# Making the Indexer's high and low parts as the features leave PSUM, instead of splitting each head's stack

## The chip, the cores and the metric

The kernel runs on one core of a Trainium2 chip. The metric is the device time of one launch in microseconds (us). The engines are named as in the profile: PE (TensorE), DVE (VectorE), ACT (ScalarE), POOL (GpSimd) and SP (SyncE, which here only issues DMAs).

## The reference

One transformer block over 1024 tokens of width 1024. The part that matters here is the Indexer of the sparse attention: it scores every key for every query, and the 256 best keys per query are kept.

```python
h = modulate(x, sh1, sc1)
proj = h @ w_in[l]
(aq, ak, av, iq, ik, iw, gq, gk, ...) = jnp.split(proj, SPLIT_OFFSETS, axis=-1)
...
iw = iw * (IDX_HEADS ** -0.5 * IDX_DIM ** -0.5)          # 16 heads of 32
idx_logits = jnp.einsum('bqhd,bsd->bqhs', iqb, ik)
score = jnp.einsum('bqh,bqhs->bqs', iwb, jax.nn.relu(idx_logits)).astype(jnp.float32)
score = jnp.where(causal[None], score, -jnp.inf)
_, sel = lax.top_k(score, topk)                           # 256 of up to 1024
```

Behind it come the attention over the selected keys, a gated linear attention (GLA), two output projections, a layer norm, a mixture of 32 experts and a last layer norm.

## The kernel before

All matmuls that must keep float32 accuracy are made of three: a number is split into a high part (what the type fp32r keeps) and a low part (the rest), and `mm3` (lines 180 to 183) adds high x high, high x low and low x high.

The first stage makes the modulated activations, transposed, as eight high and eight low tiles of 128 features x 1024 tokens (`hTh`, `hTl`). The projection stage then goes through units of 256 columns of `w_in`. `unit_load` (L214) loads a unit's raw weights by SP's queue, and `convert` splits them in four pieces, the high part on ACT (L822) and the low part on POOL (L823), while the unit before is being multiplied. The order of the units is: the keys of the Indexer with other narrow columns (`first_unit`), two units of Indexer queries (`iq_tile`, four tiles of 128 rows, that is four heads each), four gate units, then the GLA units and the rest. `feat_group` makes half a tile (128 features x 512 tokens) with eight k-steps of three matmuls into a PSUM bank of the pool `pj`, which has two.

Beside the units run threads written as Python generators: `stack_work`, `idx_work`, later `topk_work` and the GLA's. A planner's clock `now` moves by 0.64 at each k-step of `feat_group` (`spend`), and at each move every thread whose due time has come puts its next instructions into the program; each `yield` says when the thread is due again. So the order of the instructions on PE, DVE, ACT and POOL is fixed by this clock when the program is written. SP's order is left to the framework.

The Indexer's data takes this way before the change. `iq_tile` copies each half tile from PSUM to SBUF on ACT (L478) and writes the tile to a DRAM buffer `diq` (L479); `first_unit` does the same with the keys (L442, L443). A head needs its 32 query rows four times, as a stack of 128 partitions: high, high, low, low against a key stack of high, low, high, low, so that one matmul adds all products. `stack_load` loads 32 rows from DRAM four times into a raw tile of 128 partitions (L424, two buffers). `high_low` copies the whole raw tile to the stack as high part (ACT, L429) and overwrites the lower half with raw minus high (POOL, L431). The key stack `iks` is made in the same way with two such subtractions. There are six stack buffers `iqs`, so a stack is made at most five heads ahead.

`idx_work` goes through the 16 heads, and in each through the eight query blocks i with (i + 1) x 128 keys: one or two matmuls of stack and key stack into `ips` (L495, three PSUM tiles), the relu on ACT into `ixr` (L497, three buffers), and on DVE `acc += relu * weight` (L504; for head 0 L501 and L502). It is planned 25% slower than n x 1.04 ns + 0.2 us for each block, 8.0 us of the planner's clock a head. When all gate units before the GLA are placed, `finish(idx)` puts in what is left, and the top-k (L522, L525, with a last pass L528 and L531) begins on DVE beside the GLA and the other units. At the stage's end `qk_unit` makes query and key parts on ACT, POOL and DVE (L758).

The transposes of the Indexer's per-token weights (L454) and all `ips` tiles take over the PSUM banks of the pool `pjx`, in which the first query tile's two halves were begun.

Of the kernel before, what the change touches and what calls it, by code (L numbers as in the profile page):

```python
# [10 lines left out]
F32 = mybir.dt.float32  # L11
F32R = mybir.dt.float32r
# [3 lines left out]
AF = mybir.ActivationFunctionType  # L16
OP = mybir.AluOpType
# [5 lines left out]
S = 1024  # L23
# [4 lines left out]
IH = 16  # L28
# [11 lines left out]
STK_W = 4.5  # L40
STK_M = 3.5
# [117 lines left out]
def block_kernel(ctx, tc, A, out, dbg=None, stop=99):  # L159
# [4 lines left out]
    V, SC, PE, GP, SY = nc.vector, nc.scalar, nc.tensor, nc.gpsimd, nc.sync  # L164

    const = ctx.enter_context(tc.tile_pool(name="const", bufs=1))
    dram = ctx.enter_context(tc.tile_pool(name="dram", bufs=1, space=DRAM))
# [12 lines left out]
    def mm3(ps, ah, al, bh, bl, first, last):  # L180
        PE.matmul(ps, ah, bh, start=first, stop=False)  # L181
        PE.matmul(ps, ah, bl, start=False, stop=False)  # L182
        PE.matmul(ps, al, bh, start=False, stop=last)  # L183
# [168 lines left out]
    now, dve = [0.0], [0.0]  # L352
# [8 lines left out]
    def spend(dt):  # L361
        now[0] += dt
        for s in list(streams):
            while s in streams and s[1] <= now[0]:
                resume(s)

    def start(gen, delay=0.0):
        streams.append([gen, now[0] + delay])
        return streams[-1]
# [9 lines left out]
    scp = vstk.enter_context(tc.tile_pool(name="sc", bufs=1, side="right"))  # L379
    acc = [scp.tile([128, (i + 1) * 128], F32, name=f"acc{i}") for i in range(NT)]  # L380

    diq = dram.tile([544, S], F32, name="diq")
    dqk = dram.tile([1024, S], F32, name="dqk")
    dob = dram.tile([512, S], F32, name="dob")
    dvec = dram.tile([H, 384], F32, name="dvec")
# [3 lines left out]
    def feat_group(w, m0, m, half, key=None):  # L389

        ps = begun.pop((key, half), None)
        k0 = 0 if ps is None else 4
        if ps is None:
            ps = pj.tile([128, 512], F32, name="pj")[:m]
        sl = slice(half * 512, half * 512 + 512)
        for k in range(k0, KT):
            mm3(ps, w[0][:, k, m0:m0 + m], w[1][:, k, m0:m0 + m], hTh[k][:, sl], hTl[k][:, sl],
                k == 0, k == KT - 1)
            spend(0.64)
        return ps, sl  # L400
# [11 lines left out]
    c0T = wp.tile([64, S], F32, name="c0T", bufs=1)  # L412
# [4 lines left out]
    ixw = idxs.enter_context(tc.tile_pool(name="ixw", side="right", bufs=2))  # L417
    ixr = idxs.enter_context(tc.tile_pool(name="ixr", side="right", bufs=3))
    iks = ix1.tile([128, S], F32R, name="iks")

    def stack_load(src, rows):
        raw = ixw.tile([128, S], F32, name="sraw")
        for r in range(0, 128, rows):
            SY.dma_start(raw[r:r + rows], src)  # L424
        return raw

    def high_low(dst, raw, low):

        SC.activation(dst, raw, AF.Copy)  # L429
        for r in low:  # L430
            GP.tensor_tensor(dst[r], raw[r], dst[r].bitcast(F32), op=OP.subtract)  # L431

    LOW64, LOW0 = slice(64, 128), slice(0, 64)

    stacks, written, heads = {}, {}, [0]

    ipp = []

    def first_unit(w):
        for half in range(2):  # L440
            ps, sl = feat_group(w, 0, 64, half, "k")
            SC.activation(c0T[:, sl], ps, AF.Copy)  # L442
        SY.dma_start(diq[512:544], c0T[0:32])  # L443
        written["k"] = now[0]

    def stack_work():

        raw = stack_load(diq[512:544], 32)
        yield STK_0
        for half in range(2):  # L450
            ps = ipp[0].tile([128, S], F32, name="ips")[:, :512].rearrange("p (t c) -> p t c", c=128)
            for q in range(4):
                t = half * 4 + q
                PE.transpose(ps[:, q, :64], c0T[:, t * 128:(t + 1) * 128], ident[:64, :64])  # L454
            V.tensor_scalar(iwt[:, half * 4:half * 4 + 4], ps[:, :, 48:64], 16 ** -0.5 * 32 ** -0.5, None, op0=OP.mult)
            now[0] += 0.3
            yield STK_K
        high_low(iks, raw, (slice(32, 64), slice(96, 128)))
        raws_ = {}
        for h in range(IH):  # L460
            for a in (h, h + 1):
                if a < IH and a not in raws_ and (a == h or a // 4 in written):
                    while a // 4 not in written:
                        yield 0.7
                    raws_[a] = stack_load(diq[a * 32:(a + 1) * 32], 32), now[0] + (STK_M if a % 4 < 2 else 0.0)
            while now[0] < raws_[h][1] + STK_W or heads[0] < h - 5:
                yield 0.6
            stacks[h] = ixs.tile([128, S], F32R, name="iqs")
            high_low(stacks[h], raws_[h][0], (LOW64,))
            written[h, "s"] = now[0]  # L470
            yield 1.0

    def iq_tile(w, m):

        f_ = ixw.tile([128, S], F32, name="iqf")
        for half in range(2):
            ps, sl = feat_group(w, (m % 2) * 128, 128, half, "q" if m == 0 else None)
            SC.activation(f_[:, sl], ps, AF.Copy)  # L478
        SY.dma_start(diq[m * 128:(m + 1) * 128], f_)  # L479
        written[m] = now[0]  # L480
        if m == 0:
            pjx.close()
            ipp.append(idxs.enter_context(tc.tile_pool(name="ipp", bufs=3, space=PSUM)))
            start(stack_work())

    def idx_work():
        for h in range(IH):
            while (h, "s") not in written or now[0] < written[h, "s"] + 2.6:
                yield 0.6
            for i in range(NT):  # L490
                n = (i + 1) * 128
                ps = ipp[0].tile([128, S], F32, name="ips")[:, :n]
                for c in range(0, n, 512):
                    e = min(c + 512, n)
                    PE.matmul(ps[:, c:e], stacks[h][:, i * 128:(i + 1) * 128], iks[:, c:e], start=True, stop=True)  # L495
                r = ixr.tile([128, S], F32, name="ixr")[:, :n]
                SC.activation(r, ps, AF.Relu)  # L497
                sc = iwt[:, i, h:h + 1]
                if h == 0:
                    if i:  # L500
                        V.tensor_scalar(acc[i][:, :n - 128], r[:, :n - 128], sc, None, op0=OP.mult)  # L501
                    V.scalar_tensor_tensor(acc[i][:, n - 128:], r[:, n - 128:], sc, causal, op0=OP.mult, op1=OP.add)  # L502
                else:
                    V.scalar_tensor_tensor(acc[i], r, sc, acc[i], op0=OP.mult, op1=OP.add)  # L504
                now[0] += n / 2400
                yield IDXF * (n * 1.04e-3 + 0.2)
            heads[0] = h + 1
# [305 lines left out]
    def convert(cols, dst):  # L813
        raw = unit_load(cols)
        yield 6.5
        dst.append(None)
        n = raw.shape[2]
        hi = wp.tile([128, KT, 256], F32R, name="whi")[:, :, :n]
        lo = wp.tile([128, KT, 256], F32R, name="wlo")[:, :, :n]
        dst[0] = (hi, lo)  # L820
        for k in range(0, KT, 2):
            SC.activation(hi[:, k:k + 2], raw[:, k:k + 2], AF.Copy)  # L822
            GP.tensor_tensor(lo[:, k:k + 2], raw[:, k:k + 2], hi[:, k:k + 2].bitcast(F32), op=OP.subtract)  # L823
            yield 2.2
# [4 lines left out]
    def units():  # L829
        yield lambda _, w: [iq_tile(w, m) for m in range(2)], 0, [(OFF_IQ, 256)]  # L830
        yield lambda _, w: [iq_tile(w, m) for m in range(2, 4)], 0, [(OFF_IQ + 256, 256)]
        for _ in range(NG0):
            yield gate()
        yield "gla", None, None
        for p in range(2):
            yield gla_unit_a, p, [(OFF_GQ + p * 128, 128), (OFF_GK + p * 128, 128)]
            yield gla_unit_v, p, [(OFF_GV + p * 256, 256)]
            yield gla_unit_r, p, [(OFF_GR + p * 256, 256)]
            while len(gates) > (NG1 if p == 0 else 0):
                yield gate()  # L840
            if p == 0:
                yield "steps", None, None
        for u in (1, 3):
            yield qk_unit, u, [(u * 256, 256)]
        yield "values", None, None
        for u in range(2):
            yield v_unit, u, [(OFF_AV + u * 256, 256)]
        yield "attention", None, None
        for u in (0, 2):
            yield qk_unit, u, [(u * 256, 256)]  # L850

    todo_ = list(units())
    work = [u for u in todo_ if u[2] is not None]
    idx = start(idx_work(), 10.0)
    first_unit(w0)
    ready, n, topk = [wiq[0]], 0, None
    for f, a, cols in todo_:
# [13 lines left out]
        else:  # L871
            n += 1
            nxt = []
            s = start(convert(work[n][2], nxt)) if n < len(work) else None
# [324 lines left out]
    rows = {}  # L1199
# [734 lines left out]
```

## Time and profile before

| | |
|---|---|
| median of 3 runs | 1417.73 us (1417.11 to 1421.07) |
| profiled execution | 1416.12 us |
| its span | 1414.3 us |
| mean granted clock of PE | 0.966 of full speed |
| busy: PE, DVE, ACT, POOL | 1314.1 (93%), 1167.2 (83%), 730.0 (52%), 484.0 (34%) us |
| DMA | 262.69 MB, mean 186 GB/s |

The profile is of one execution. Times in it count from the start of its span. A busy time is the union of the instructions of an engine, which overlap a little at their ends; matmuls are pipelined, and their ends are modelled, so their distance from start to start tells more than their length. The granted clock is a share of full speed: 1.00 is 2.4 GHz, and a mean between 0.5 and 1.00 is a mix with 1.2 GHz. The projection stage lies between about 65 and 662 us, and its Indexer part between 65 and 248 us.

### The profile page before, as it was taken

What the parts mean: (1) busy time and instruction counts of PE and PEld (TensorE: products, weight loads), DVE (VectorE), ACT (ScalarE), POOL (GpSimd) and SP (SyncE); (2) the same over time, 40 slices, a digit from 0 to 9 for tenths busy, and PEclk for the clock granted to TensorE, in tenths of its full rate; (3) what the DMA queues carried; (4) which work ended last, traced back from release to release, by engine and by line L of the source; (5) the groups of instructions that cost most, each with busy time, mean ns of one, the idle gap of its engine ahead of it and who ended that gap; (6) DMA issues with size and microseconds to landing.
All of it is one profiled execution on the core that took longest, in us unless ns stands there. A gap on an engine that the chain in (4) does not pass through costs nothing. (4 is left out here: it accounts for less than half of the span.)

```text
span 1414.3 us, 21326 instructions
## 1 busy us (share of the span) xinstructions
PE 1314.1 (93%) x7535; PEld 1057.3 (75%) x7535; DVE 1167.2 (83%) x2127; ACT 730.0 (52%) x1321; POOL 484.0 (34%) x492
## 2 busy tenths in 40 slices
PE   4988999999999999998989999989869999999975
PEld 2566778897889788996447768989758888888842
DVE  5638998997989799993878758788889999999947
ACT  2446776343234322223566644322348988898834
POOL 2465441275227522132455424311211222222114
PEclk9999999999999999999999999999859999999987
DMA  8454332121302123202774456837459999999964
GB/s 279 163 157 141 119 93 87 46 61 35 115 31 64 56 92 108 72 31 89 284 268 133 137 169 223 293 123 255 150 183 370 371 387 365 371 345 366 372 248 176
DMA packets 133375, 262.69 MB, mean 186 GB/s; under 512 B 20656, under 2 KB 71144, under 8 KB 131216
## 3 DMA queue, kind: packets, MB, share of 16 engines
q1 hardware_dynamic: 122336, 243.17, 49.3%
q0 software_dynamic: 9216, 16.80, 3.2%
q8 instruction: 60, 0.98, 0.3%
q10 hardware_dynamic: 1712, 1.32, 0.3%
q14 instruction: 51, 0.42, 0.1%
HBM read 229.61 MB, written 48.39 MB: 197 GB/s over the span
## 5 line engine op out<-in xcount | busy, mean ns | idle before, releaser
L1562 DVE TENSOR_TENSOR elo<-pg,ehi 128x1024 fp32r<-128x1024 f32 x188 | 219.1, 1220 | 17.5 <-ACT ehi L1557 13.3
L181 PE MATMUL pj<-hTh,whi 128*128 128x512 f32 (+1 forms) x528 | 211.3, 400 | 0.0
L182 PE MATMUL pj<-hTl,whi 128*128 128x512 f32 (+1 forms) x528 | 207.5, 393 | 1.9 <-DVE hTl L307 1.2
L183 PE MATMUL pj<-hTh,wlo 128*128 128x512 f32 (+1 forms) x528 | 207.2, 392 | 0.0
L1557 ACT ACTIVATE ehi<-pg 128x1024 fp32r<-128x1024 f32 x192 | 190.2, 1075 | 0.9 <-PE eph L183 0.9
L823 POOL TENSOR_TENSOR wlo<-raw,whi 128x512 fp32r<-128x512 f32 x84 | 111.8, 1344 | 208.8 <-ACT whi L822 199.8
L525 DVE MATCH_REPLACE8 acc<-m,acc 128x1024 f32<-128x1024 f32 (+2 forms) x192 | 167.8, 886 | 0.0
L522 DVE MAX8 m<-acc 128x8 f32<-128x1024 f32 (+2 forms) x192 | 163.0, 889 | 0.0
L504 DVE SCALAR_TENSOR_TENSOR acc<-ixr,iwt,acc 128x128 f32<-128x128 f32 (+3 forms) x120 | 127.2, 1115 | 15.5 <-ACT ixr L497 14.8
L181 PEld LDWEIGHTS pj<-hTh,whi 128*128 128x128 f32 (+1 forms) x528 | 98.9, 187 | 22.8 <-issue 1.9
L182 PEld LDWEIGHTS pj<-hTl,whi 128*128 128x128 f32 (+1 forms) x528 | 99.1, 188 | 22.4 <-DVE hTl L307 2.7
L183 PEld LDWEIGHTS pj<-hTh,wlo 128*128 128x128 f32 (+1 forms) x528 | 98.9, 187 | 22.7 <-issue 0.6
L181 PE MATMUL pj<-whi,hTh 128*128 128x256 f32 x384 | 111.8, 291 | 0.0
L182 PE MATMUL pj<-wlo,hTh 128*128 128x256 f32 x384 | 108.6, 283 | 0.0
L183 PE MATMUL pj<-whi,hTl 128*128 128x256 f32 x384 | 108.5, 283 | 0.0
L181 PE MATMUL eph<-ehi,xh 128*128 128x512 f32 x256 | 105.5, 412 | 0.0
L182 PE MATMUL eph<-elo,xh 128*128 128x512 f32 x256 | 102.6, 401 | 1.1 <-DVE elo L1567 1.1
L497 ACT ACTIVATE ixr<-ips 128x128 f32<-128x128 f32 (+7 forms) x128 | 80.3, 656 | 44.4 <-DVE acc L504 24.2
L183 PE MATMUL eph<-ehi,xl 128*128 128x512 f32 x256 | 102.3, 400 | 0.0
L1581 POOL DMA_INDIRECT xg<-dh,gidx x32 | 34.3, 1071 | 161.4 <-PE etp L1677 139.8
L181 PEld LDWEIGHTS pj<-whi,hTh 128*128 128x128 f32 x384 | 73.4, 191 | 6.8 <-issue 5.5
L181 PE MATMUL yps<-whi,pg 128*128 128x256 f32 x256 | 74.7, 292 | 0.2 <-ACT pg L1242 0.2
(321 smaller groups left out, 3195.2 us busy)
## 6 DMA issues: line engine op xcount, KB each, us to landing
pg<-in_w_exp_gate_dram SPq DMA_DIRECT2D x64, 512.0 KB, 13.1
pg<-in_w_exp_up_dram SPq DMA_DIRECT2D x64, 512.0 KB, 13.9
pg<-in_w_exp_down_dram SPq DMA_DIRECT2D x32, 1024.0 KB, 15.8
raw<-in_w_in_dram SPq DMA_DIRECT2D x20, 1024.0 KB, 5.4
wada<-in_w_ada_dram SPq DMA_DIRECT2D x16, 1024.0 KB, 5.7
dgate<-gate SPq DMA_DIRECT2D x48, 256.0 KB, 2.1
gate<-dgate SPq DMA_DIRECT2D x48, 256.0 KB, 3.3
sraw<-diq SPq DMA_DIRECT2D x68, 128.0 KB, 2.7
```

The source lines that it names most:

```text
L181: PE.matmul(ps, ah, bh, start=first, stop=False)
L182: PE.matmul(ps, ah, bl, start=False, stop=False)
L183: PE.matmul(ps, al, bh, start=False, stop=last)
L497: SC.activation(r, ps, AF.Relu)
L504: V.scalar_tensor_tensor(acc[i], r, sc, acc[i], op0=OP.mult, op1=OP.add)
L522: V.max(m, acc[i])
L525: V.match_replace(acc[i], m, acc[i], -3.0e38)
L823: GP.tensor_tensor(lo[:, k:k + 2], raw[:, k:k + 2], hi[:, k:k + 2].bitcast(F32), op=OP.subtract)
L1557: SC.activation(h3, src, AF.Copy)
L1562: V.tensor_tensor(*args, op=OP.subtract)
L1581: GP.indirect_dma_start(out=x, out_offset=None, in_=dh2, in_offset=bass.IndirectOffsetOnAxis(ap=gi, axis=0), bounds_check=S - 1, oob_is_er ...
```

## The change

The high and low parts are made once, as the features leave PSUM: `features` copies a half tile to the high part (ACT) and subtracts it from PSUM into the low part (DVE). Both go to DRAM, in two buffers `diq`, for high and low. `stack_load` then loads 32 rows of one or the other straight into the four quarters of a stack; `high_low` and the raw tiles are gone. The conditions under which `stack_work` and `idx_work` go on are changed with it: a stack is loaded as soon as its tile is written and its buffer is free by the plan, and a head begins when the planner's clock has passed the load by `STK_W` (4.5), and `STK_M` (3.5) more for the first two heads of a tile.

```diff
-    diq = dram.tile([544, S], F32, name="diq")
+    diq = [dram.tile([544, S], F32, name=f"diq{x}") for x in "hl"]
...
-    def stack_load(src, rows):
-        raw = ixw.tile([128, S], F32, name="sraw")
-        for r in range(0, 128, rows):
-            SY.dma_start(raw[r:r + rows], src)
-        return raw
-
-    def high_low(dst, raw, low):
-
-        SC.activation(dst, raw, AF.Copy)
-        for r in low:
-            GP.tensor_tensor(dst[r], raw[r], dst[r].bitcast(F32), op=OP.subtract)
-
-    LOW64, LOW0 = slice(64, 128), slice(0, 64)
+    def stack_load(dst, r, parts):
+
+        for i, x in enumerate(parts):
+            SY.dma_start(dst[32 * i:32 * i + 32].bitcast(F32), diq[x][r:r + 32])
+
+    def features(ps, hi, lo):
+        SC.activation(hi, ps, AF.Copy)
+        V.tensor_tensor(lo, ps, hi.bitcast(F32), op=OP.subtract)
...
     def first_unit(w):
+        hl = [ixw.tile([128, S], F32R, name="iqf" + x)[:32] for x in "hl"]
         for half in range(2):
             ps, sl = feat_group(w, 0, 64, half, "k")
+            features(ps[:32], hl[0][:, sl], hl[1][:, sl])
             SC.activation(c0T[:, sl], ps, AF.Copy)
-        SY.dma_start(diq[512:544], c0T[0:32])
+        for d, x in zip(diq, hl):
+            SY.dma_start(d[512:544], x.bitcast(F32))
         written["k"] = now[0]
 
     def stack_work():
 
-        raw = stack_load(diq[512:544], 32)
+        stack_load(iks, 512, (0, 1, 0, 1))
...
-        high_low(iks, raw, (slice(32, 64), slice(96, 128)))
-        raws_ = {}
         for h in range(IH):
-            for a in (h, h + 1):
-                if a < IH and a not in raws_ and (a == h or a // 4 in written):
-                    while a // 4 not in written:
-                        yield 0.7
-                    raws_[a] = stack_load(diq[a * 32:(a + 1) * 32], 32), now[0] + (STK_M if a % 4 < 2 else 0.0)
-            while now[0] < raws_[h][1] + STK_W or heads[0] < h - 5:
+            while h // 4 not in written or heads[0] < h - 5:
                 yield 0.6
             stacks[h] = ixs.tile([128, S], F32R, name="iqs")
-            high_low(stacks[h], raws_[h][0], (LOW64,))
-            written[h, "s"] = now[0]
+            stack_load(stacks[h], h * 32, (0, 0, 1, 1))
+            written[h, "s"] = now[0] + (STK_M if h % 4 < 2 else 0.0) + STK_W
             yield 1.0
 
     def iq_tile(w, m):
 
-        f_ = ixw.tile([128, S], F32, name="iqf")
+        hl = [ixw.tile([128, S], F32R, name="iqf" + x) for x in "hl"]
         for half in range(2):
             ps, sl = feat_group(w, (m % 2) * 128, 128, half, "q" if m == 0 else None)
-            SC.activation(f_[:, sl], ps, AF.Copy)
-        SY.dma_start(diq[m * 128:(m + 1) * 128], f_)
+            features(ps, hl[0][:, sl], hl[1][:, sl])
+        for d, x in zip(diq, hl):
+            SY.dma_start(d[m * 128:(m + 1) * 128], x.bitcast(F32))
         written[m] = now[0]
...
     def idx_work():
         for h in range(IH):
-            while (h, "s") not in written or now[0] < written[h, "s"] + 2.6:
+            while (h, "s") not in written or now[0] < written[h, "s"]:
                 yield 0.6
```

## Rows read from the trace of the kernel before

**Rows 1.** Busy time by stretch: stretch, its length, engines' busy time, clock, DMA share, GB/s.
```profile
88.00:125.00 37.00, 31.11 (x129) 24.00 (x129) 31.04 (x29) 23.69 (x38) 24.31 (x12) 0.95 0.48 138
125.00:165.00 40.00, 35.75 (x154) 28.56 (x155) 35.67 (x35) 26.79 (x44) 16.78 (x8) 0.96 0.53 158
165.00:205.00 40.00, 39.06 (x177) 31.04 (x176) 37.96 (x33) 29.27 (x50) 19.88 (x11) 1.00 0.28 86
205.00:250.00 45.00, 44.86 (x207) 36.96 (x206) 37.12 (x44) 30.45 (x50) 9.87 (x10) 1.00 0.27 84
250.00:440.00 190.00, 188.18 (x1214) 161.35 (x1212) 168.73 (x326) 72.90 (x143) 86.79 (x96) 1.00 0.19 59
440.00:645.00 205.00, 205.00 (x1252) 174.97 (x1253) 184.19 (x368) 58.24 (x130) 73.01 (x92) 1.00 0.21 68
```

**Rows 2.** Waits of PE, 65 to 250 us: total, times, longest.
```profile
PE ips L495 <- ACT ixr L497: 10.7, 11, 2.9
PE ips L495 <- POOL iqs L431: 1.5, 1, 1.5
```

**Rows 3.** Waits of ACT in the same stretch.
```profile
ACT ixr L497 <- DVE acc L504: 24.2, 23, 3.0
...
ACT whi L822 <- DMA raw<-in_w_in_dram: 3.6, 1, 3.6
```

**Rows 4.** DVE's accumulations: all (busy, mean ns), then one head from 209 us.
```profile
L504 DVE SCALAR_TENSOR_TENSOR acc<-ixr,iwt,acc 128x128 f32<-128x128 f32 (+3 forms) x120 | 127.2, 1115 | 15.5 <-ACT ixr L497 14.8
...
209.02 6.28 DVE L504 SCALAR_TENSOR_TENSOR acc<-ixr,iwt,acc 128x640 f32<-128x640 f32 x8 [0.81 <-ACT ixr L497]
```

**Rows 5.** Timeline of POOL and DVE: start, length.
```profile
177.95 2.83 POOL L431 TENSOR_TENSOR iqs<-sraw,iqs 64x1024 fp32r<-64x1024 f32 x1 [0.50 <-ACT iqs L429]
178.46 2.47 DVE L504 SCALAR_TENSOR_TENSOR acc<-ixr,iwt,acc 128x128 f32<-128x128 f32 x1
...
213.16 0.34 DVE L504 SCALAR_TENSOR_TENSOR acc<-ixr,iwt,acc 128x128 f32<-128x128 f32 x1
```

**Rows 6.** Groups by line of POOL and ACT, 65 to 250 us.
```profile
L431 POOL TENSOR_TENSOR iqs<-sraw,iqs 64x1024 fp32r<-64x1024 f32 x16 | 41.3, 2590 | 41.4 <-ACT iqs L429 41.1
L823 POOL TENSOR_TENSOR wlo<-raw,whi 128x512 fp32r<-128x512 f32 x24 | 35.1, 1471 | 47.0 <-ACT whi L822 38.1 <-PE ips L454 8.2 <-POOL iqs L431 0.3
...
L429 ACT ACTIVATE iqs<-sraw 128x1024 fp32r<-128x1024 f32 x16 | 17.1, 1068 | 3.5 <-DMA sraw<-diq 3.5
...
L478 ACT ACTIVATE iqf<-pj 128x512 f32<-128x512 f32 x8 | 4.8, 599 | 8.0 <-PE pj L183 8.0
```

**Rows 7.** Groups by line of DVE, whole span (etp and yps are in PSUM).
```profile
L1679 DVE TENSOR_TENSOR xl<-etp,xh 128x512 fp32r<-128x512 f32 x64 | 41.1, 683 | 1.9 <-ACT xh L1678 1.9
...
L1232 DVE TENSOR_TENSOR gate<-gate 128x512 f32<-128x512 f32 x16 | 17.5, 1091 | 0.5
...
L1231 DVE TENSOR_TENSOR gate<-yps,gate 128x512 f32<-128x512 f32 x16 | 10.9, 681 | 3.5 <-PE yps L183 3.5
```

**Rows 8.** Timeline of PE, the stage's last matmuls.
```profile
660.87 0.39 PE L183 MATMUL pj<-hTh,wlo 128*128 128x512 f32 x1
...
661.55 0.39 PE L183 MATMUL pj<-hTh,wlo 128*128 128x512 f32 x1
```

**Rows 9.** SP's issues, timeline from 82 us, and DMA issues (KB, us to landing).
```profile
83.72 0.37 SPq L479 DMA_DIRECT2D diq<-iqf  x1
85.79 0.40 SPq L214 DMA_DIRECT2D raw<-in_w_in_dram  x1
...
raw<-in_w_in_dram SPq DMA_DIRECT2D x20, 1024.0 KB, 5.4
...
diq<-iqf SPq DMA_DIRECT2D x4, 512.0 KB, 3.0
```

**Rows 10.** Timeline of DVE at the stage's end.
```profile
647.96 2.69 DVE L531 TENSOR_SCALAR acc<-acc 128x1024 f32<-128x1024 f32 x6
...
663.26 0.69 DVE L758 TENSOR_TENSOR akl<-gate,akh 128x512 fp32r<-128x512 f32 x1 [4.74 <-ACT akh L757]
```

## The prediction

> **What bounds the kernel now.** I read five views, from wide to narrow. First the busy shares by stretch [rows 1]: from 205 us on TensorE (PE) is busy 44.86 of 45, then 188.18 of 190, then 205.00 of 205, so the projection stage is bound by PE, and what this stage gives up must come from its front. There, where the Indexer runs beside the projections, PE is idle for 5.89 us of 88 to 125, 4.25 of 125 to 165 and 0.94 of 165 to 205, and the granted clock is 0.95 and 0.96. Second, PE's waits there [rows 2]: 10.7 us in 11 waits for the relu on ACT (L497), and 1.5 us once for a stack's low part from POOL (L431). Third, what the relu waits for [rows 3]: 24.2 us for the accumulation on DVE (L504). So PE waits for ACT, and ACT for DVE; DVE is busy 31.04 of 37, 35.67 of 40 and 37.96 of 40 [rows 1]. Fourth, why DVE is slow [rows 4, 5]: 120 accumulations hold it for 127.2 us, 8.5 a head, but a head takes 6.28 us in a stretch that POOL hardly disturbs. A 128x128 one takes 0.34 us by itself and 2.47 us when it begins 0.5 us into an L431 on POOL: it stands still until POOL is done. The subtraction on POOL that the change deletes is thus what starves DVE.
>
> **What the loss is worth.** PE's waits are 10.7 + 1.5 = 12.2 us [rows 2]. A granted 0.95 over 37 us and 0.96 over 40 us [rows 1] is a mix of 2.4 and 1.2 GHz and lost 1.85 + 1.6 = 3.45 us of full-speed time; PE had been idle ahead of both, so I count it with the waits. Together 15.65 us, the most that the change can win in this stretch.
>
> **Removed.** On POOL 16 subtractions of 2.59 us and two like them for the key stack, some 46 us; on ACT 16 copies of 1.07 us and one for the key stack, 18 us [rows 6]. Their buffers go too, so the stack loads no longer wait for POOL. What that frees on DVE: L504 exceeds 15 heads of 6.28 us by 33 us; L431 is 54% of POOL's subtractions between 65 and 250 (41.3 us beside 35.1 of L823, which stays), so 18 us by shares; the other bound is 15 stacks at the 2.13 us of [rows 5], 32 us. I take 25, the middle.
>
> **Added.** Ten subtractions on DVE, eight of 128x512 and two of 32x512, from PSUM. The nearest row is L1679, the same operation and shape from PSUM, 0.683 us [rows 7], 6.8 us in all; L1232, both inputs in SBUF, takes 1.091 us in the stretch where L1231, one input in PSUM, takes 0.681. That is the upper bound (10.9 us), zero the lower (if DVE is idle there); I take 0.683. The Trainium skill ("SBUF — State Buffer", section "Who interferes with whom") holds that a VectorE operation with at most one SBUF input does not contend with GpSimd, while one with two is shut out until the other ends. L1231 beside L1232 agrees. By the rule the new operations are free of POOL; if they were not, the four in the tight stretch below would cost 0.41 us more each and the sum would be 10 us instead of 11.6. ACT has two 32x512 copies more, at most the 0.6 us each of L478 [rows 6], ahead of the first head, where it follows PE: I take nothing (1.2 us if all of it stood on the path). Five writes to DRAM more, of 512 KB or less, meet DMA engines that are 27 to 53% busy [rows 1]: nothing for bandwidth; their latency is below.
>
> **Moved.** Followed through the code by the planner's own clock (0.64 for one k-step of three matmuls), the first head's matmuls are put in 33 k-steps after the stage's begin where they stood at 38, since a stack needs no conversion any more; by the end of the second unit (64 steps) 3.5 heads are placed instead of 3. The last head ends at step 183 instead of 188 of 192; the rest of the plan is the same.
>
> **The tight stretch** is steps 33 to 64. One k-step takes 0.68 us (the third matmul begins at 660.87 and again at 661.55) [rows 8], a head's twelve matmuls about 2.5 us (estimate: 12 of 0.19 to 0.23): PE needs 31 x 0.68 + 3.5 x 2.5 = 29.8 us. DVE needs 3.5 heads x 6.28 = 22.0, four new subtractions 2.7, and about 1.1 us for each of four L823 beside it (half of 2.13, as L823 is about half as long [rows 6]), 4.4: 29.1 us. DVE is no longer over PE's time, but at 98% of it. In 165 to 205 DVE was 95% busy and PE idle 2.4% [rows 1]; the same share of 30 us is 0.7 us, and I take 1. In later units DVE needs 2.7 x 6.28 + 4.4 = 21 us in some 28.5 us of PE, 74%, less than between 205 and 250 (82%), where PE idled 0.14 us [rows 1]: 0.3 us.
>
> **New waits.** (a) The transposes (L454) take over the bank of the first unit's second half, which is now released by DVE's subtraction and not by the copy: PE stands 0.68 us longer, with every matmul of the next groups behind it (bounds 0.68 and 1.09) [rows 7]. (b) On SyncE's queue the load of stack 4 stands ahead of the raw weights of the next unit and waits for two writes that begin about 1.3 us later than the one write does now (0.6 for the copy of its second half [rows 6], 0.68 for the subtraction) and take 3.0 us to land; now the raw load issues 2.1 us after that write [rows 9]. The weights land 5.4 us after issue [rows 9], and ACT has waited 3.6 us for such a load already [rows 3], partly because POOL's key-stack work held the buffer back, which goes. Behind a waiting ACT stand the relus, and PE covers three rows of those. I take 2 us (0, if the raw load is ordered ahead, to 4).
>
> **Sum.** 15.65 - 0.7 - 1.3 - 2.0 = 11.6 us. It carries through: PE sets the pace to 661.55 [rows 8], while the top-k on DVE, the other long thread, ends its list at 650.65 [rows 10] and begins earlier by as much or more. After this stage no instruction differs. The profiled execution takes 1416.12 us (span 1414.3 and 1.8 around it), so 1404.5; it is 1.6 us under the median of 1417.73, where the same gain gives 1406.1.
>
> **Rivals.**
> A. Only the later waits go. The tight stretch stays bound by DVE and the late weights, so it keeps its 5.89 + 1.85 us; of 15.65 some 7.9 remains, less 0.7 and 0.3: 6.9 us, 1411. For it: DVE at 98% in my sum, two writes in the path. Against: the L431 that stop DVE there are gone.
> B. The gain is given back before the stage ends, since something else releases the next stage: 1417.7. For it: DVE is busy 168.73 of 190 and 184.19 of 205 [rows 1], and the top-k must finish first. Against: it has 11 us of slack at the end [rows 8, 10], and starts earlier.
> C. Slower, by SyncE's queue: a stack load now waits for a head's last matmul (six stack buffers), and a unit's raw weights behind it come late. A head is planned every 8.0 units, 8.5 us; the convert thread waits 6.5 units, 6.9 us, from issue to first use, 1.5 us more than the landing [rows 9], so each of five raw loads may be 7 us late, of which PE covers 3: 20 us lost against 13.65 won (15.65 less 0.7 and 1.3), 6 slower: 1424. It decides when a waiting stack load stands directly ahead of most raw loads. Against: by the planner's clock only stack 4 does; the others wait for heads that are done one k-step before.
> D. The change doesn't do what it says, POOL's lock being L823's work: then DVE gains nothing and pays 6.8 us. Against it [rows 5]. I count it with B.
>
> **Chances.** Forecast (gain 8 to 15.65) 0.62; A 0.18; B with D 0.13; C 0.07. A change under 0.3% (4.3 us) can't be told from none here. Faster by more than that: forecast and A, 0.80; within it: B, 0.13; slower: C, 0.07. The range reaches from the whole 15.65 us (1402) over A to a gain of 4 (1414): it leaves out B and C, 2 in 10.
>
> **What would show it.** Right: no L431 and L429; L504 at about 102 us for 120 (127.2 less 25) and near 6.3 a head wherever L823 rests; PE's waits for L497 under 4 us; the last L504 ending some 15 us earlier (11.6 and five k-steps); L758's last near 652 instead of 663.26 [rows 10]. A: idle PE in 83 to 113 as now. B: the stretch shorter, the stage's end where it was. C: ACT waiting for raw loads at every unit's start. Wrong at the root: L504 still at 8.5 us a head with L431 gone.

## The result and the profile after

The changed kernel takes 1401.73 us (median of 4 runs, 1400.98 to 1403.06) where the kernel before takes 1419.40 beside it: a ratio of 0.9895, interval 0.9869 to 0.9922. Two more comparisons on other chips gave 0.9918 (0.9891 to 0.9945) and 0.9916 (0.9889 to 0.9943). By these ratios the gain is 12 to 15 us; the medians alone lie 17.7, 12.5 and 12.8 us apart. The profiled span falls from 1414.3 to 1401.3 us. The forecast was 11.6 us, 1406 with a range from 1402: the first median lies 0.3 us below it, the later ones (1402.88 and 1404.35) in it.

The busy time by stretch of the changed kernel, with the same columns as [rows 1]:

```profile
88.00:125.00 37.00, 32.94 (x144) 26.92 (x143) 25.16 (x35) 22.22 (x36) 6.08 (x4) 0.95 0.56 167
125.00:165.00 40.00, 39.69 (x185) 32.73 (x184) 32.31 (x36) 27.38 (x50) 11.36 (x7) 1.00 0.47 144
165.00:205.00 40.00, 40.00 (x186) 33.14 (x186) 33.18 (x38) 28.42 (x48) 9.01 (x5) 1.00 0.40 119
205.00:250.00 45.00, 45.00 (x205) 37.30 (x204) 39.94 (x55) 22.73 (x39) 12.48 (x12) 1.00 0.19 60
250.00:440.00 190.00, 188.22 (x1265) 162.34 (x1264) 164.28 (x325) 73.82 (x148) 92.19 (x105) 1.00 0.18 57
440.00:645.00 205.00, 205.00 (x1204) 174.00 (x1203) 177.28 (x353) 57.31 (x126) 63.13 (x79) 1.00 0.21 67
```

From 125 us on PE is dense: 185 and 186 matmuls in 40 us instead of 154 and 177 [rows 1]. POOL falls from 24.31 to 6.08 us in the first stretch. One stretch still has a hole, 88 to 125, with the clock again at 0.95 (1.00 and 0.95 in the two other profiles of this kernel). Next, waits between 65 and 250 us, PE's and then ACT's:

```profile
PE ips L487 <- ACT ixr L489: 4.4, 2, 4.1
PE ips L452 <- DVE iqfl L428: 0.7, 1, 0.7
...
ACT ixr L489 <- PE ips L487: 32.9, 64, 1.2
...
ACT ixr L489 <- DVE acc L496: 7.8, 9, 1.9
ACT whi L814 <- DMA raw<-in_w_in_dram: 6.3, 2, 5.1
```

PE waited 11 times for the relu [rows 2], now twice; the relu's waits for DVE fall from 24.2 us [rows 3] to 7.8, and what ACT mostly waits for is PE, as it should be in a stage that PE bounds. DVE's and POOL's groups by line in that stretch (busy, mean ns):

```profile
L496 DVE SCALAR_TENSOR_TENSOR acc<-ixr,iwt,acc 128x128 f32<-128x128 f32 (+3 forms) x120 | 107.3, 933 | 23.9 <-ACT ixr L489 23.1
...
L428 DVE TENSOR_TENSOR iqfl<-pj,iqfh 128x512 fp32r<-128x512 f32 (+1 forms) x10 | 6.9, 686 | 19.8 <-ACT iqfh L427 19.8
...
L815 POOL TENSOR_TENSOR wlo<-raw,whi 128x512 fp32r<-128x512 f32 x28 | 43.0, 1548 | 135.4 <-ACT whi L814 115.3 <-PE ips L487 20.0
```

The accumulations (L504 before, L496 now) hold DVE for 107.3 instead of 127.2 us [rows 4]; the new subtractions cost 6.9. The last accumulation of the kernel before, then the changed kernel's and the end of its stage on DVE, from the timelines:

```profile
246.60 1.28 DVE L504 SCALAR_TENSOR_TENSOR acc<-ixr,iwt,acc 128x1024 f32<-128x1024 f32 x1 [0.79 <-ACT ixr L497]
...
230.92 1.28 DVE L496 SCALAR_TENSOR_TENSOR acc<-ixr,iwt,acc 128x1024 f32<-128x1024 f32 x1 [0.79 <-ACT ixr L489]
...
650.95 0.69 DVE L750 TENSOR_TENSOR akl<-gate,akh 128x512 fp32r<-128x512 f32 x1 [4.74 <-ACT akh L749]
```

The accumulations end 15.7 us earlier. The stage's last L750 begins at 650.95 where it began at 663.26 [rows 10]: 12.3 of the 13.0 us are won by then.

### The profile page after: what moved, and what is told of

Its sections match the earlier page's. It is cut to its first block, busy times and chain, and to the rows that moved or that the text cites. A ratio compares the mean times of both kernels' runs of the same rounds, so it can differ in the third digit from the quotient of the medians.

```text
span 1401.3 us, 21266 instructions
## 1 busy us (share of the span) xinstructions
PE 1308.8 (93%) x7535; PEld 1057.7 (75%) x7535; DVE 1145.8 (82%) x2137; ACT 717.4 (51%) x1306; POOL 440.5 (31%) x474
## 5 line engine op out<-in xcount | busy, mean ns | idle before, releaser
L815 POOL TENSOR_TENSOR wlo<-raw,whi 128x512 fp32r<-128x512 f32 x84 | 114.5, 1378 | 289.0 <-ACT whi L814 268.8
L496 DVE SCALAR_TENSOR_TENSOR acc<-ixr,iwt,acc 128x128 f32<-128x128 f32 (+3 forms) x120 | 107.3, 933 | 23.9 <-ACT ixr L489 23.1
```

## The experiments

Three theories. P: POOL's subtractions shut DVE's accumulations out, and their deletion is the gain. A: the gain is ACT's, which no longer copies stacks between the relus. O: it is the other order, with heads placed earlier and stacks loaded ahead. Later two more, on the stall that is left: Q (the early burst of stack loads fills the DMA engines) and R (the raw weights are issued too late).

**The changed kernel again**, to have it beside the next three on one chip.

> The changed kernel once more, so that the next three stand beside it on one chip. All theories: about 0.9895 of the kernel before, some 13 to 15 us faster.

Ratio 0.9918 (0.9891 to 0.9945), 1402.88 us.

**POOL's work put back.** The subtraction's result goes to a tile that nobody reads.

```diff
+    junk = ix1.tile([128, S], F32, name="junk")
...
             stack_load(stacks[h], h * 32, (0, 0, 1, 1))
+            again = stacks[h][64:128].bitcast(F32)
+            GP.tensor_tensor(junk[64:128], again, again, op=OP.subtract)
```

> The changed kernel plus one 64x1024 subtraction on POOL for each stack, which reads the loaded stack twice and writes to a spare tile that nobody reads. Theory P (POOL's subtractions shut DVE's accumulations out, and that was the loss): L496 goes back from 107 to 125 us or more for 120, PE's waits for the relu from 4.4 to 8 or more, and 7 to 11 of the 13 us are given back (1408 to 1413). Theory A (ACT's copies were the loss) and theory O (the other order and the earlier stacks are the gain): within 3 us of the changed kernel.

Ratio 0.9998 (0.9981 to 1.0016), 1415.05 us: all of the gain is gone, more than expected. PE's waits:

```profile
PE ips L490 <- ACT ixr L492: 11.2, 8, 4.0
PE pj L183 <- POOL wlo L818: 2.3, 2, 1.3
```

The groups of DVE's accumulations and of the added work on POOL:

```profile
L499 DVE SCALAR_TENSOR_TENSOR acc<-ixr,iwt,acc 128x128 f32<-128x128 f32 (+3 forms) x120 | 126.1, 1105 | 15.4 <-ACT ixr L492 15.1
...
L463 POOL TENSOR_TENSOR junk<-iqs 64x1024 f32<-64x1024 f32 x16 | 33.1, 2067 | 66.6 <-DMA iqs<-diql 59.8 <-DVE iqfl L429 6.3
```

The accumulations are back at 126.1 us and PE's waits for the relu at 11.2, nearly as in [rows 2, 4]. PE's wait for POOL is a side effect: the added subtraction waits for its stack's load, with the weights' low parts queued behind it. So this run alone overstates P a little.

**The converse: the kernel before without POOL's subtraction.** The key stack is made as before.

```diff
-            high_low(stacks[h], raws_[h][0], (LOW64,))
+            high_low(stacks[h], raws_[h][0], ())
```

> The kernel before without POOL's low subtraction on the 16 head stacks: their lower halves keep the high part. Order, raw tiles, SyncE's loads and ACT's copies stay. Theory P: 8 to 11 us faster than before (1407 to 1411), L504 from 127 to about 105 us. Theory A and theory O: under 3 us, since neither ACT nor the order changes.

Ratio 0.9918 (0.9891 to 0.9945), 1403.46 us: the same as the changed kernel beside it. That is 11.9 us below the kernel before on this chip, a little more than I expected. PE's waits:

```profile
PE ips L495 <- ACT ixr L497: 3.3, 3, 1.8
```

The accumulations:

```profile
L504 DVE SCALAR_TENSOR_TENSOR acc<-ixr,iwt,acc 128x128 f32<-128x128 f32 (+3 forms) x120 | 104.0, 903 | 28.4 <-ACT ixr L497 27.6
```

All 17 ACT copies, the raw tiles and the old order are still in this kernel. Theories A and O have nothing left to explain, beyond what the intervals of some 4 us either way leave open.

**ACT's work put back.** Two kernels, each with one of the added lines: the first copies the loaded stack, the second a tile that has long been there. The spare tile `junk` is made as above, here and in the next run.

```diff
             stack_load(stacks[h], h * 32, (0, 0, 1, 1))
+            SC.activation(junk, stacks[h].bitcast(F32), AF.Copy)    # act_back
+            SC.activation(junk, hTh[0].bitcast(F32), AF.Copy)       # act_free
```

> The changed kernel plus one 128x1024 copy on ACT for each stack, of the loaded stack into a spare tile that nobody reads; 16 of 1.07 us. Theory A: most of the 13 us is given back. Theory P: at most 3 us, since ACT is busy 109 of 185 us in this stretch; L496 stays at 107 us. Theory O: nothing.

Ratio 1.024 (1.021 to 1.0269), 1448.69 us, against every theory. ACT's and PE's waits say why:

```profile
ACT junk L462 <- DMA iqs<-diql: 58.0, 14, 11.4
...
PE ips L489 <- ACT ixr L491: 32.9, 11, 9.7
```

The copies stood in ACT's queue waiting for their loads, with the relus behind them. The run tested a wait and not the copies' work, so it was made anew:

> The changed kernel plus one 128x1024 copy on ACT at each stack's place, now of an activation tile that has long been there, so that the copy waits for nothing; act_back's copies stood waiting for their stack's load with the relus behind them. Theory P: within 4 us of the changed kernel (0.992), as 16 copies of 1.07 us fit beside PE. Theory A: 8 to 13 us of the gain given back.

Ratio 0.9902 (0.9875 to 0.9929), 1402.09 us, with PE's waits for the relu at 3.3 us: 17 us of copies on ACT cost nothing that can be measured. Theory A falls.

**POOL busy, but without reading.**

```diff
             stack_load(stacks[h], h * 32, (0, 0, 1, 1))
+            for _ in range(3):
+                GP.memset(junk, 0.0)
```

> The changed kernel plus three memsets on POOL of a spare 128x1024 tile for each stack, 2 to 3 us a stack, about what pool_back's subtraction took; a memset reads nothing. Theory P with the shared reading port (what shuts DVE out is that both read SBUF): L496 stays near 107 us for 120 and the time within 4 us of the changed kernel. Rival (POOL's being busy is enough, through any sharing with DVE or by delaying the low parts of the weights): 8 us or more given back, as in pool_back.

Ratio 0.9902 (0.9874 to 0.993), 1402.79 us, beside 0.9916 for the changed kernel on that chip (below).

```profile
L463 POOL MEMSET junk<- 128x1024 f32 x48 | 47.0, 979 | 2.2
...
L499 DVE SCALAR_TENSOR_TENSOR acc<-ixr,iwt,acc 128x128 f32<-128x128 f32 (+3 forms) x120 | 105.8, 919 | 25.1 <-ACT ixr L492 24.2
```

POOL is busy 47.0 us more, against 33.1 in the run that gave all back, and the accumulations stay at 105.8. In the trace 33 of the 120 ran mainly beside memsets, and they are as short as undisturbed ones: 0.34 to 0.35 us for 128x128. So it is not POOL's being busy that stops the accumulations, which read two inputs from SBUF. What the subtraction does and the memset doesn't is read SBUF; no other operation without reads was tried.

Another operation of DVE did stand still for the memsets: the seven TENSOR_SCALAR of head 0, which read one tile from SBUF. Their group here, then in the changed kernel on the same chip:

```profile
L496 DVE TENSOR_SCALAR acc<-ixr,iwt 128x128 f32<-128x128 f32 (+6 forms) x7 | 6.7, 1028 | 0.7 <-ACT ixr L492 0.7
...
L493 DVE TENSOR_SCALAR acc<-ixr,iwt 128x128 f32<-128x128 f32 (+6 forms) x7 | 3.4, 486 | 2.9 <-ACT ixr L489 2.9
```

One of them, and accumulations of 128 to 384 columns, beside three memsets:

```profile
97.17 3.34 POOL L463 MEMSET junk<- 128x1024 f32 x3
97.32 1.28 DVE L496 TENSOR_SCALAR acc<-ixr,iwt 128x896 f32<-128x896 f32 x1 [0.22 <-ACT ixr L492]
...
98.79 1.32 DVE L499 SCALAR_TENSOR_TENSOR acc<-ixr,iwt,acc 128x128 f32<-128x128 f32 x3
```

Each of the seven ended only after the memset that was running when it began, and all took longer than in the changed kernel (this one 1.28 instead of 0.69 us). They are few, 3.3 us in all, and the time does not show it.

**The new subtractions made twice.**

```diff
         V.tensor_tensor(lo, ps, hi.bitcast(F32), op=OP.subtract)
+        V.tensor_tensor(lo, ps, hi.bitcast(F32), op=OP.subtract)
```

> The changed kernel with each of the ten new subtractions on DVE made twice, 6.8 us more on DVE. By my sum they are hidden: 0.68 us more at the transposes behind the first query tile, and up to 2 in the tight stretch, so 0 to 3 us slower than the changed kernel. Rival (DVE sets the pace of the Indexer's part, and each microsecond on it counts): 6 to 7 us slower.

Ratio 0.9915 (0.9888 to 0.9942), 1403.63 us: 1.5 us above act_free on that chip, and between 0.7 below and 1.9 above the three medians of the changed kernel. PE's waits, with 1.7 us instead of 0.7 at the transposes:

```profile
PE ips L488 <- ACT ixr L490: 2.8, 2, 1.8
PE ips L453 <- DVE iqfl L429: 1.7, 1, 1.7
```

So the work on DVE is hidden but for the one place that was named, as far as a few us can be told; the 6 to 7 us of the rival did not come.

**The heads as late as before**, beside a third measurement of the changed kernel.

```diff
-STK_W = 4.5
+STK_W = 7.7
```

> The changed kernel, so that the next three stand beside it on one chip: 0.990 to 0.992 of the kernel before.

> The changed kernel with STK_W 7.7 instead of 4.5: a head begins 3.2 units of the planner's clock later after its load, so that head 0 stands where it stood in the kernel before. Theory P: within 2 us of the changed kernel. Theory O (placing the heads 3.4 us earlier is part of the gain): 3 us slower.

The changed kernel 0.9916 (0.9889 to 0.9943), 1404.35 us; the late heads 0.991 (0.9882 to 0.9939), 1402.81 us. Where the heads stand in the plan makes no difference that can be measured. The intervals are some 4 us wide either way, so this run alone does not exclude the 3 us of theory O, and in its trace PE waits a little more for the relu (5.8 us in 4 waits); that the old order gives the whole gain without the subtraction is the stronger evidence.

**The stall that is left.** Two kernels load fewer stacks ahead.

```diff
-            while h // 4 not in written or heads[0] < h - 5:
+            while h // 4 not in written or heads[0] < h - 2:      # ahead_2
+            while h // 4 not in written or heads[0] < h - 1:      # ahead_1
```

> The changed kernel with stacks loaded at most two heads ahead instead of five. The one stall left, 3 to 4 us of PE near 95 us, is ACT waiting for the third unit's raw weights, which were issued at 86 us and needed some 10 us, with the DMA engines full from 75 to 95 us. Theory Q (the early burst of stack loads fills the DMA engines): the raw weights land 2 to 4 us earlier, 2 to 4 us faster than the changed kernel. Theory R (the raw load is late by its issue, behind the writes of the second query tile and its buffer's release): the stall stays, same time.

> The changed kernel with stacks loaded one head ahead. Theory Q: the stall goes wholly, 3 to 5 us faster than the changed kernel, unless heads then wait for their stacks. Theory R: the same time, or slower where a head waits.

Ratios 0.9882 (0.9856 to 0.9907), 1399.03 us, and 0.9863 (0.9835 to 0.989), 1396.55 us. No changed kernel ran on that chip; its three ratios were 0.9895 to 0.9918. The changed kernel first, its timeline: SP's issue of the raw weights, the load of stack 4 behind it, and ACT's first use of the weights.

```profile
85.99 0.38 SPq L214 DMA_DIRECT2D raw<-in_w_in_dram  x1
88.05 1.48 SPq L424 DMA_DIRECT2D iqs<-diqh  x2
...
96.44 0.63 ACT L814 ACTIVATE whi<-raw 128x512 fp32r<-128x512 f32 x1 [5.13 <-DMA raw<-in_w_in_dram]
```

The stretches around (the last two columns are DMA share and GB/s):

```profile
75.00:85.00 10.00, 10.00 (x46) 8.29 (x45) 1.27 (x2) 2.51 (x5) 2.54 (x2) 1.00 1.01 241
85.00:95.00 10.00, 9.46 (x45) 7.53 (x43) 4.56 (x14) 3.80 (x6) 0.00 (x0) 1.00 1.01 293
95.00:105.00 10.00, 6.48 (x23) 5.28 (x24) 5.98 (x9) 6.73 (x13) 4.00 (x3) 0.83 0.28 78
```

The same two views of ahead_1:

```profile
84.43 0.49 SPq L214 DMA_DIRECT2D raw<-in_w_in_dram  x1
...
91.66 0.63 ACT L814 ACTIVATE whi<-raw 128x512 fp32r<-128x512 f32 x1 [1.49 <-DMA raw<-in_w_in_dram]
```

```profile
75.00:85.00 10.00, 10.00 (x47) 8.35 (x46) 1.98 (x5) 3.27 (x7) 2.54 (x2) 1.00 0.53 137
85.00:95.00 10.00, 9.58 (x45) 7.63 (x44) 5.83 (x16) 6.27 (x12) 1.56 (x2) 1.00 0.94 266
95.00:105.00 10.00, 10.00 (x48) 8.33 (x47) 9.94 (x12) 7.43 (x14) 4.81 (x3) 1.00 0.46 150
```

In the changed kernel the DMA engines are full from 75 to 95 us, and the raw weights take 10.5 us from issue to first use. With one head ahead the engines have room, the weights need 7.2 us, ACT's wait falls from 5.13 to 1.49 us, and between 95 and 105 PE makes 48 matmuls instead of 23, at the full clock. The first use comes 4.8 us earlier, 3.2 by the shorter transfer (Q) and 1.6 by the issue, of which 1.1 is only that this execution reached the stage earlier (its first features are copied at 63.57 us instead of 64.65). The other two profiles of the changed kernel have 9.5 and 10.1 us from issue to first use, and ahead_2 has 7.7. So Q holds, and R has next to no share, some 0.5 us. How deep the hole is differs from one execution of the changed kernel to the next; in the profile of its second measurement the same stretch is:

```profile
95.00:105.00 10.00, 9.01 (x42) 7.55 (x43) 9.66 (x12) 8.15 (x16) 6.01 (x4) 1.00 0.46 159
```

**Both stalls taken away.**

```diff
-STK_0 = 0.0
+STK_0 = 1.0
...
-            while h // 4 not in written or heads[0] < h - 5:
+            while h // 4 not in written or heads[0] < h - 1:
```

> ahead_1 with STK_0 1.0 instead of 0.0, which puts the transposes of the token weights one k-step later, behind the subtraction that releases their bank. Theory: PE's last two stalls in 65 to 250 us, 0.7 and 0.4 us, go, and the kernel is 4 to 7 us faster than the changed one. Rival: the 0.7 us only moves; then it equals ahead_1, 3 to 6 us faster than the changed one.

Ratio 0.9854 (0.9827 to 0.9882), 1395.68 us, 8.7 us below the changed kernel's 1404.35 on the same chip, and the fastest median measured. PE has no wait left between 65 and 250 us. The stretches of [rows 1], the first two:

```profile
88.00:125.00 37.00, 37.00 (x172) 30.73 (x171) 30.99 (x42) 26.55 (x45) 8.89 (x7) 1.00 0.59 176
125.00:165.00 40.00, 40.00 (x186) 33.25 (x186) 33.21 (x36) 27.72 (x47) 9.21 (x6) 1.00 0.50 148
```

The stage's last subtraction on DVE, 8.4 us before the changed kernel's, from the timeline:

```profile
642.58 0.69 DVE L750 TENSOR_TENSOR akl<-gate,akh 128x512 fp32r<-128x512 f32 x1 [4.74 <-ACT akh L749]
```

Whether the transposes' 0.7 us add to ahead_1 can't be told: 0.9854 and 0.9863 lie within each other's intervals.

## Why the prediction was right, step by step

**The chain PE, ACT, DVE, POOL** was read rightly. Putting POOL's subtraction back took all of the gain away, taking it out of the kernel before gave all of it, and neither ACT's copies nor the heads' place moved the time.

**What was at stake was sized too small.** I took waits plus clock, 15.65 us. By that account the changed kernel won 8.7 us (waits from 12.2 to 5.1, clock from 3.45 to 1.85), and it won 12 to 15. The matmul counts give another sum: with the dense pace of the last kernel (172 in 37 us, 186 in 40 us, so 0.215 us each), the kernel before is short of 43, 32 and 9 matmuls in the three stretches from 88 to 205 [rows 1], 18.1 us. Counted by kind, since a 128-column matmul takes 0.06 us there from start to start and a 512-column one 0.23, it is 18.1 too. PE's modelled ends probably cover part of a delayed start; that was not tried. In any case idle time understates here what a stalled PE loses. The changed kernel is short of 28 and 1, 6.2 us; the difference of 11.9 lies by the measured gain.

**What was left over was sized too small too**, 4.0 us instead of 6.2 (3.4 and 6.2 in the other two profiles). In this profile the two errors nearly cancel, so it is in part luck that 11.6 us came out so near. Of its terms, the transposes' wait came out at 0.7 us as forecast. The tight stretch did not stay at DVE's limit: DVE was busy 25.16 of 37 us, and 30.99 of 37 when the raw weights came in time, 84%; in the 30 us of that sum, from 83 us, 23.50, 78% and not 98%. The 4.4 us put down to L823 beside the heads were too many: accumulations there exceed undisturbed ones of their shape by 1.3 to 2.3 us. Of PE's 4.4 us for the relu, 0.3 are left for the two terms of 1 and 0.3. The raw weights were the miss: PE stood 4.1 us for them (3.1 and 3.7 in the other two profiles), in this profile it then ran at a lower clock, and I had taken 2 of 0 to 4. The reason given was wrong as well. I put stack 4's load ahead of the raw weights in SP's queue; the trace has the raw load at 85.99 us, ahead of it, at nearly the time it had before (85.79 [rows 9]). What was full was the DMA engines, with stacks 0 to 3 and two writes for one. I had priced the added writes by the share of 27 to 53% in long stretches and dismissed bandwidth; in 75 to 95 us the share was 1.01.

**DVE's freed time** was 19.9 us (127.2 less 107.3) where I took 25 between bounds of 18 and 32; the shares by POOL's time were the better bound. The accumulations at 107.3 missed the 102 in the list of signs, as did PE's waits for the relu, 4.4 where I wrote under 4. The new operations cost 0.686 us each (L428; 0.676 to 0.692 over all ten), those that met a subtraction on POOL too (at 97.59 and 105.83 us). The Trainium skill ("SBUF — State Buffer", "Who interferes with whom") has two conditions that I left out: an operation with at most one SBUF input is free of GpSimd only "outside the 2-port perf modes", and one with two "contends with a GpSimd instruction that reads SBUF". The traces agree where they try it: the new subtractions, with one input in SBUF and one in PSUM, were not delayed, and the accumulations were stopped by a POOL operation that reads and not by a memset. That one SBUF input alone does not free an operation is shown by the seven TENSOR_SCALAR, 6.7 us instead of 3.4 beside memsets; in which mode they ran no run here shows.

**Carrying through** held: 12.3 us at the stage's end, 13.0 at the kernel's. Rival A came in one half: the first stretch kept a hole, 4.06 us idle instead of 5.89 and the clock at 0.95 again, from the late weights, but not from DVE, and the gain was not the 6.9 us it gave. B and C did not come: the top-k did not hold the end, and ACT waited for raw weights twice in all (6.3 us), not at every unit.

## What to carry to other kernels

Before moving work off a busy engine, look at which engine makes it slow: a group whose mean is far above its own undisturbed row is waiting inside its instructions, and no wait shows in the views. Splitting work once at the source rather than once per use is worth what it takes off the engine in the way: here the copies saved on ACT gave nothing that can be measured, and the subtractions taken off POOL gave all of it. When loads can run further ahead, check what else must land in those microseconds: here one stack ahead instead of five, with the transposes a step later, won 8.7 us on top of the change.

## What the runs showed beyond that

- A memset on POOL, 47.0 us of it, left DVE's two-input accumulations alone (105.8 us), while 33.1 us of subtractions held them up by some 19 us. The one-input TENSOR_SCALAR stood still for the memset too (6.7 instead of 3.4 us for seven).
- The weights' low parts on POOL, which stay, still hold up the accumulations that they meet: 128x128 ones take up to 1.39 us beside L815 instead of 0.34.
- One instruction that waits for a DMA, put in ACT's queue ahead of relus, cost 45 us in 16 uses, 14 of which waited (1448.69 against 1402 to 1404), though the copy itself costs nothing that can be measured.
- Behind the one stall of the changed kernel the granted clock fell to 0.83 in 95 to 105 us, a mix of 2.4 and 1.2 GHz, in two of its three profiles; in the third (42 matmuls in that stretch) and with the stall gone it stayed at 1.00.
